# A Griffin-style hybrid layer on one core: other SBUF places for two groups of weights, a prologue that finishes token tile 0 first, and one rounding of a projection block moved

## The chip, the cores and the metric

The kernel runs on one core of one Trainium2 chip. The metric is the device time of one execution in microseconds. The core's engines are called PE (matmul; PEld is its weight load), DVE (vector), ACT (scalar), POOL (GpSimd) and SP (which here only issues DMAs). Each works through its own instructions in order, and they wait for each other through semaphores.

## What is computed

One layer on 512 tokens of width 1024, in float32. The reference, cut to what matters:

```python
h = rms_norm(x, mix_norm_pre)
xa, ga, q, k, v, f_logit, g_a, g_b = split(h @ w_in)
y_a = gelu(ga) * rg_lru(causal_dwconv(xa))            # 1280 wide
y_b = forgetting_attention(q, k, v, f_logit)          # 16 heads of 64
merged = sigmoid(g_a + b0) * (y_a @ w_proj_a) + sigmoid(g_b + b1) * (y_b @ w_proj_b)
x = x + rms_norm(merged @ w_out, mix_norm_post)
h = rms_norm(x, ffn_norm_pre)
gate, val = split(causal_dwconv(h @ w_up))            # 2 x 3072
x = x + rms_norm((gelu(gate) * val) @ w_down, ffn_norm_post)
```

## The kernel before

Every large product is made of three matmuls in the 32-bit format `float32r`. Each operand is split into a rounded high part and the rest: high times high, high times low, low times high (`mm3`, L216 to L219). A block of weights therefore arrives by DMA into a tile `raw`; ACT rounds it into `wh` (L172) and DVE, in the prologue POOL, subtracts to get `wl` (L175). `wpool` holds four of each. `fetch` works through the list `order` of weight blocks, and `unit(name, ahead)` takes a block and has the ones after it loaded and rounded. Outside of the blocks under `manual_schedule` a scheduler sets the place of each instruction on its engine; `tc.issue_after(i)` makes what is written under it stand behind `i`.

**Prologue** (L557 to L670, order by hand). The 512 tokens are four tiles of 128 (`xts`). For each tile ACT squares and sums (`sumsq`), DVE multiplies by the root and by the gains (`scaled(t, g)`, g being a half of the 1024 columns; result `xn`), PE transposes each half by four matmuls with the identity (`turn(t, g)`, L245, tile `tr_p`), ACT rounds the transposed half into `hh` (`evac_hi`, L249) and DVE puts the rest into `hl` (`evac_lo`, L253). The gains reach all 128 partitions by a matmul of a row of ones with the row `gone` (L590), in plain float32. `spin` is a matmul of the identity with itself, whose result nobody reads. The first useful product is `half(0, X)` (L229 to L232): block `xa0` with the first 256 tokens, X; Y are the last 256. It reads `hh` and `hl` of tiles 0 and 1, and the rounded `wh_xa0` and `wl_xa0`.

**Gates** (L906 to L960). The blocks `ma0` to `mb7` are made in pairs by Strassen's scheme, seven products of 12 matmuls of 256 columns each (`product`, L408 to L421). Their operands: products 1 and 2 (`p12`) take the plain weights `gmh0`/`gml0` (pool `gsplit0`) and `hh`/`hl`; product 3 takes `gmh1`/`gml1` (pool `gsplit1`) and the token sums `gsh3`; products 5, 6 and 7 take sums of weights (`gth`/`gtl`, in `wpool`) and token sums `gsh`/`gsl`; product 4 takes `gth`/`gtl` and `hh`/`hl`. In the steady order of `period` (L443) they run as 5, 6, 4 of the pair before, 3, `p12` of the next pair, 7. In PE's instructions the weights are the stationary operand and the tokens are streamed.

**Attention** (L1070 to L1109). A loop over eight pairs of heads, p = 0 to 7: scores of pair p from `q` and `k`, each split by `halves` into a high part on ACT (L970) and the rest on DVE (L971); transposes `pt` of pair p-1 with their copies by ACT (L1030) and DVE (L1031); `av` of pair p-1. In the last rounds the products of `pb`, the projection of the attention's result, fill PE. `pb_part(e, ks)` adds to block e, and at its first call takes its weights with one block ahead, so `pb_part(2, ...)` is what has `pb3` rounded.

**Up** (L1162 to L1476). The blocks `up0`, `up24`, `up1`, `up25`, `up2`, `up26` come first, each as two halves of 24 matmuls of 256 columns (X, later Y), with `h2h`/`h2l`; the weights of `up0` and `up24` have a pool of their own (`wfirst`). The other 42 blocks are 21 Strassen pairs as in the gates, there with the plain weights `mh0`, `mh1` and the sums `th`. **Down** (L1382 on) follows, with Strassen again.

The helper `offset(stack, n, side)` (L85) takes n bytes per partition at a place, so that what is put behind it moves by n. By the sizes of the pools the byte places within 512 of the operands that matter are: `hh`, `hl`, `gth`, `gtl`, `th`, `tl` at 0; `gsh`, `gsl`, `h2h`, `h2l`, `sh`, `sl` at 448; `gmh0`/`gml0` at 448; `gmh1`/`gml1`, `up0` and `up24` at 0; in the up stage `mh0` at 0 and `mh1` at 416. A block of 128 weights is 512 bytes wide and a stretch of 256 tokens 1024, so a place stays the same through a product.

Of the kernel before, what the change touches and what calls it, by code (L numbers as in the profile page):

```python
# [8 lines left out]
F32 = mybir.dt.float32  # L9
F32R = mybir.dt.float32r  # L10
BF16 = mybir.dt.bfloat16
AF = mybir.ActivationFunctionType
ALU = mybir.AluOpType
# [50 lines left out]
def kernel(  # L64
# [421 lines left out]
    with ExitStack() as rg:  # L486
        rt, ixt, tt = {}, {}, {}
        last_act = [None]
        with ExitStack() as r0:
# [68 lines left out]
            with tc.tile_pool(name="pre", bufs=2, side="right", reuse_waits="tile") as pre, ExitStack() as wp:  # L558
# [6 lines left out]
                gone = pre.tile([1, D + P], F32, name="gone", bufs=1)  # L565
                pool.memset(gone[:, D:], 1.0)
                act.dma_start(gone[:, :D], gains[0:1, :])
# [21 lines left out]
                for i in range(2):  # L589
                    pe.matmul(pgain[i], gone[:, D:], gone[:, 512 * i : 512 * i + 512], start=True, stop=True)  # L590
# [18 lines left out]
                def scaled(t, g):  # L609
                    c = HALVES[g]  # L610
                    dve.scalar_tensor_tensor(out=xns[t][:, c], in0=xts[t][:, c], scalar=rss[t], in1=pgain[g],
                                             op0=ALU.mult, op1=ALU.mult)

                def turn(t, g):
                    ptr[t, g] = turn_block(xns[t], t, g, "p")
# [11 lines left out]
                scaled(0, 0)  # L627
                sumsq(1)
                us[0].hi()
                us[0].lo(pool)  # L630
                scaled(1, 0)
                turn(0, 0)
                spin(3)
                turn(1, 0)
                scaled(0, 1)
                turn(0, 1)
                evac_hi(0, 0)
                evac_lo(0, 0)
                scaled(1, 1)
                turn(1, 1)  # L640
                evac_hi(1, 0)
                evac_lo(1, 0)
                evac_hi(0, 1)
                evac_lo(0, 1)
                evac_hi(1, 1)
                evac_lo(1, 1)
                half(0, X)
# [259 lines left out]
    with ExitStack() as g2:  # L907
# [9 lines left out]
        hfstk.close()  # L917
        st0pool = splitstk.enter_context(tc.tile_pool(name="gsplit0", bufs=2, side="right", reuse_waits="tile"))
        offset(splitstk, 448, "right")
# [43 lines left out]
    with ExitStack() as at:  # L963
# [47 lines left out]
        def pt(p, pts):  # L1011
# [10 lines left out]
            for j in range(2):  # L1022
                h = 2 * p + j
                th = apool.tile([P, PO[NT]], F32R, tag="PTh", name=f"PTh{h}")
                tl = apool.tile([P, PO[NT]], F32R, tag="PTl", name=f"PTl{h}")
                thv, tlv = (a.rearrange("p (i h c) -> p i h c", h=2, c=HD) for a in (th, tl))
                for i0, i1, src, o in ((0, 8, tbs[j], 0), (8, 10, rest, P * j)):
                    for half in range(2):
                        ps = src[half][:, o : o + (i1 - i0) * HD].rearrange("p (i c) -> p i c", c=HD)
                        act.copy(thv[:, i0:i1, half], ps)  # L1030
                        dve.tensor_tensor(out=tlv[:, i0:i1, half], in0=ps, in1=thv[:, i0:i1, half].bitcast(F32), op=ALU.subtract)  # L1031
                res.append((th, tl))
# [23 lines left out]
        def pb_part(e, ks):  # L1056
            if e not in pb:
                pb[e] = bank(f"pb{e}")
                pbw[e] = unit(f"pb{e}", 1)
            wh, wl = pbw[e]  # L1060
            for k in ks:
                mm3(pb[e], wh[:, k], wl[:, k], yb[k][:, 0], yb[k][:, 1], k == 0, k == KD - 1)

        rounded = []
# [76 lines left out]
    offset(fstk, 96)  # L1141
# [19 lines left out]
    with ExitStack() as mix:  # L1161
        wfpool = mix.enter_context(tc.tile_pool(name="wfirst", bufs=2, reuse_waits="tile"))  # L1162
        npool = mix.enter_context(tc.tile_pool(name="norm", bufs=2, reuse_waits="tile"))
        special["up0"] = special[f"up{JF}"] = wfpool
# [129 lines left out]

    ypool = fstk.enter_context(tc.tile_pool(name="ff", bufs=3, reuse_waits="tile"))
# [429 lines left out]
```

## Time and profile before

| | us |
|---|---|
| three runs | 915.5, 914.26, 915.56; median 915.5 |
| the profiled execution: its own time | 915.62 |
| its span, from the first to the last instruction | 913.8 |
| around the span | 1.8 |
| mean granted clock of PE | 0.998 |

The page's other lines stand in the prediction where they are used. Its times are microseconds from the span's start unless a column says ns. In a timeline a row gives start, duration, engine, line, operation, what it writes and reads, and in brackets how long the engine had been idle and what ended that. Matmuls are pipelined: a row's duration is longer than the distance to the next matmul's start, and it is the distances that add up to the time. L12 is line 12 of the kernel before.

### The profile page before, as it was taken

How to read it: one execution, taken by the hardware profiler on the slowest of the kernel's cores; microseconds unless marked ns; L12 is line 12 of the kernel's file. 1: busy time of each engine (PE TensorE's matmuls, PEld its weight loads, DVE VectorE, ACT ScalarE, POOL GpSimd, SP SyncE). 2: the span in 40 equal slices, each digit the busy share in tenths (PEclk: the TensorE clock that was granted, in tenths of full speed). 3: DMA queues.
4: the chain of work that ended last, by engine and by line, in shares of the span. 5: the costliest groups of instructions: out<-in, count | busy, mean ns of one | idle time of the engine just before them, and what ended most of it. 6: DMA issues, size and time to landing. Idle time of an engine off the chain costs nothing.

```text
span 913.8 us, 15945 instructions
## 1 busy us (share of the span) xinstructions
PE 904.4 (99%) x5906; PEld 805.5 (88%) x5906; DVE 726.0 (79%) x1197; ACT 601.6 (66%) x1041; POOL 218.9 (24%) x281
## 2 busy tenths in 40 slices
PE   8999999999999999999999999999999999999997
PEld 7988888887899998888888889999999999988886
DVE  4966359737777649888878588989999999889897
ACT  6565496423377757677654477878888888677664
POOL 4134444534111112212104200132323223100000
PEclk9999999999999999999999999999999999999999
DMA  7677669989968767435424654468988888699764
GB/s 261 234 214 207 191 166 274 256 229 182 212 164 198 199 222 261 180 128 174 139 93 156 208 180 160 116 174 201 231 227 209 236 210 211 205 397 328 243 200 148
DMA packets 72048, 187.86 MB, mean 206 GB/s; under 512 B 7265, under 2 KB 27793, under 8 KB 71586
## 3 DMA queue, kind: packets, MB, share of 16 engines
q1 hardware_dynamic: 47648, 127.72, 41.9%
q0 software_dynamic: 24176, 58.99, 29.8%
q8 instruction: 46, 0.75, 0.3%
q14 instruction: 32, 0.26, 0.1%
q10 hardware_dynamic: 146, 0.14, 0.0%
HBM read 150.69 MB, written 35.73 MB: 204 GB/s over the span
## 4 chain that ended last, share of the span: by engine, by line
PE 96%; DVE 1%; DMA 1%; ACT 1%; SPq 0%; issue 0%; DVEq 0%; ACTq 0%
PE up L421 7%; PE up L419 7%; PE up L418 7%; PE dn L1434 4%; PE dn L1432 4%; PE dn L1433 4%; PE pa L217 2%; PE ga L218 2%; PE ga L217 2%; PE pa L219 2%; PE pa L218 2%; PE ga L219 2%; PE k L217 2%; PE q L217 2%; PE wo L1151 2%; PE pb L217 2%
## 5 line engine op out<-in xcount | busy, mean ns | idle before, releaser
L1309 DVE SCALAR_TENSOR_TENSOR u<-up,cpt,u 128x511 f32<-128x511 f32 x96 | 71.3, 746 | 3.5 <-ACT u L1303 1.8
L362 POOL DMA_DIRECT2D ml<-raw_up x41 | 35.3, 861 | 152.6 <-ACT ml L361 89.5
L1434 PE MATMUL dn<-wh_dn,al 128*128 128x512 f32 (+1 forms) x180 | 67.7, 376 | 0.0
L1433 PE MATMUL dn<-wl_dn,ah 128*128 128x512 f32 (+1 forms) x180 | 67.5, 375 | 0.0
L1432 PE MATMUL dn<-wh_dn,ah 128*128 128x512 f32 (+1 forms) x180 | 67.5, 375 | 0.0
L419 PE MATMUL up<-sl,th 128*128 128x256 f32 x252 | 60.2, 276 | 0.0
L418 PE MATMUL up<-sh,th 128*128 128x256 f32 x252 | 60.2, 276 | 0.0
L175 DVE TENSOR_TENSOR wl_dn<-raw_dn,wh_dn 128x1024 fp32r<-128x1024 f32 x42 | 51.3, 1222 | 9.3 <-ACT wh_dn L172 9.2
L172 ACT CAST wh_dn<-raw_dn 128x1024 fp32r<-128x1024 f32 x42 | 44.1, 1050 | 21.2 <-PE dn L1434 7.3
L1303 ACT ACTIVATE u<-up,cpt 128x512 f32<-128x512 f32 x48 | 36.9, 778 | 21.6 <-PE up L421 11.6
L324 DVE TENSOR_TENSOR tl<-t,th 128x1024 fp32r<-128x1024 f32 x42 | 51.0, 1217 | 0.0
L419 PEld LDWEIGHTS up<-sl,th 128*128 128x128 f32 x252 | 47.3, 188 | 0.0
L418 PEld LDWEIGHTS up<-sh,th 128*128 128x128 f32 x252 | 47.3, 188 | 0.0
L1317 POOL TENSOR_TENSOR yf<-u,u 128x512 f32<-128x512 f32 x23 | 31.4, 1365 | 63.3 <-issue 48.8
L400 ACT CAST th<-t 128x1024 fp32r<-128x1024 f32 x42 | 43.8, 1045 | 3.3 <-DVE t L324 0.8
L418 PE MATMUL up<-h2h,mh 128*128 128x256 f32 x168 | 40.2, 276 | 0.0
L419 PE MATMUL up<-h2l,mh 128*128 128x256 f32 x168 | 40.2, 276 | 0.0
L1434 PEld LDWEIGHTS dn<-wh_dn,al 128*128 128x128 f32 x180 | 33.9, 188 | 6.8 <-DVE al L324 0.7
L1433 PEld LDWEIGHTS dn<-wl_dn,ah 128*128 128x128 f32 x180 | 33.9, 188 | 6.1
L1432 PEld LDWEIGHTS dn<-wh_dn,ah 128*128 128x128 f32 x180 | 33.9, 188 | 6.0
L421 PE MATMUL up<-sh,tl 128*128 128x256 f32 x252 | 38.8, 276 | 0.0
L998 ACT ACTIVATE P<-P,mx 128x384 f32<-128x384 f32 (+3 forms) x64 | 35.2, 553 | 4.2 <-DVE mx L993 3.3
(717 smaller groups left out, 3239.1 us busy)
## 6 DMA issues: line engine op xcount, KB each, us to landing
raw_up<-in_w_up_dram SPq DMA_DIRECT2D x48, 512.0 KB, 5.4
td<-in_w_down_dram POOLq DMA_DIRECT2D x36, 512.0 KB, 6.0
raw_dn<-td SPq DMA_DIRECT2D x24, 512.0 KB, 5.2
B<-cnd POOLq DMA_DIRECT2D x16, 640.0 KB, 5.5
ml<-raw_up POOLq DMA_DIRECT2D x20, 512.0 KB, 5.8
raw_dn<-in_w_down_dram SPq DMA_DIRECT2D x18, 512.0 KB, 4.3
raw_wo<-in_w_out_dram SPq DMA_DIRECT2D x16, 512.0 KB, 3.9
td<-td POOLq DMA_DIRECT2D x12, 512.0 KB, 10.6
```

The costliest lines, as they stand in the source:

```text
L172: act.copy(self.wh, self.raw)
L175: engine.tensor_tensor(out=self.wl, in0=self.raw, in1=self.wh.bitcast(F32), op=ALU.subtract)
L217: pe.matmul(dst, ah, bh, start=first, stop=False)
L324: dve.tensor_tensor(out=out, in0=a, in1=b, op=ALU.subtract)
L400: act.copy(self.th[i], self.t[i])
L418: pe.matmul(dst, wh[:, k], ah[:, k], start=first and k == 0, stop=False, skip_group_check=True)
L419: pe.matmul(dst, wh[:, k], al[:, k], start=False, stop=False, skip_group_check=True)
L421: pe.matmul(dst, wl[:, k], ah[:, k], start=False, stop=k == KH - 1, skip_group_check=True)
L1309: dve.scalar_tensor_tensor(out=c[:, s:], in0=ps[:, : S - s], scalar=col(C_CFW + 3 * e + j), in1=c[:, s:], op0=ALU.mult, op1=ALU.add)
L1432: pe.matmul(d[:, x], ah[:, k, tok], wh[:, k, x], start=first, stop=False, skip_group_check=True)
L1433: pe.matmul(d[:, x], ah[:, k, tok], wl[:, k, x], start=False, stop=False, skip_group_check=True)
L1434: pe.matmul(d[:, x], al[:, k, tok], wh[:, k, x], start=False, stop=last, skip_group_check=True)
```

## The change

Four places of the program differ. In the prologue, the gains go to the partitions as two `float32r` products (high part and rest, split by DVE) in place of one plain one; tile 0 is scaled, turned and rounded whole before tile 1; and the first half of `xa0` runs all its high-by-high matmuls, then high-by-low, then low-by-high. In the gates the pool `gsplit0` moves by 384 bytes and the distance between the two pools shrinks as much, so that `gmh0`/`gml0` come to place 64 within 512 and `gmh1`/`gml1` stay. For the up stage the two first blocks get a pool each with 96 bytes between them, and `x2t` moves down by 96, so that `up0` comes to place 416 and `up24` stays at 0 (it moves by 4096). In the attention the load and rounding of `pb3` are put behind the last of ACT's copies of `pt(6)`.

```diff
-                gone = pre.tile([1, D + P], F32, name="gone", bufs=1)
-                pool.memset(gone[:, D:], 1.0)
-                act.dma_start(gone[:, :D], gains[0:1, :])
+                gone = pre.tile([1, D], F32, name="gone", bufs=1)
+                act.dma_start(gone, gains[0:1, :])
...
-                for i in range(2):
-                    pe.matmul(pgain[i], gone[:, D:], gone[:, 512 * i : 512 * i + 512], start=True, stop=True)
+                one = xpool.tile([P, S], F32R, tag="xc", name="one")[0:1, :P]
+                pool.memset(one.bitcast(F32), 1.0)
+                for i, c in enumerate(HALVES):
+                    gh, gl = (xpool.tile([P, S], F32R, tag=x, name=f"gain_{x}{i}")[0:1] for x in ("xh", "xl"))
+                    dve.tensor_copy(out=gh, in_=gone[:, c])
+                    dve.tensor_tensor(out=gl, in0=gone[:, c], in1=gh.bitcast(F32), op=ALU.subtract)
+                    for j, g in enumerate((gh, gl)):
+                        pe.matmul(pgain[i], one, g, start=j == 0, stop=j == 1)
...
                 sumsq(0)
                 scaled(0, 0)
+                scaled(0, 1)
+                turn(0, 0)
+                turn(0, 1)
+                spin(3)
                 sumsq(1)
+                evac_hi(0, 0)
+                evac_hi(0, 1)
                 us[0].hi()
                 us[0].lo(pool)
-                scaled(1, 0)
-                turn(0, 0)
-                spin(3)
-                turn(1, 0)
-                scaled(0, 1)
-                turn(0, 1)
-                evac_hi(0, 0)
-                evac_lo(0, 0)
-                scaled(1, 1)
-                turn(1, 1)
-                evac_hi(1, 0)
-                evac_lo(1, 0)
-                evac_hi(0, 1)
-                evac_lo(0, 1)
-                evac_hi(1, 1)
-                evac_lo(1, 1)
-                half(0, X)
+                for g in range(2):
+                    scaled(1, g)
+                    turn(1, g)
+                for g in range(2):
+                    evac_lo(0, g)
+                for g in range(2):
+                    evac_hi(1, g)
+                    evac_lo(1, g)
+                wh, wl = us[0].parts()
+                for w, h in ((wh, hh), (wh, hl), (wl, hh)):
+                    for k in range(KD):
+                        pe.matmul(pss[0][:, X], w[:, k], h[:, k, X], start=w is wh and h is hh and k == 0, stop=w is wl and k == KD - 1)
...
         hfstk.close()
+        offset(splitstk, 384, "right")
         st0pool = splitstk.enter_context(tc.tile_pool(name="gsplit0", bufs=2, side="right", reuse_waits="tile"))
-        offset(splitstk, 448, "right")
+        offset(splitstk, 64, "right")
         st1pool = splitstk.enter_context(tc.tile_pool(name="gsplit1", bufs=2, side="right", reuse_waits="tile"))
...
-                        act.copy(thv[:, i0:i1, half], ps)
+                        copied[p] = act.copy(thv[:, i0:i1, half], ps)
...
-                pbw[e] = unit(f"pb{e}", 1)
+                with ExitStack() as held_back:
+                    if e == 2:
+                        held_back.enter_context(tc.issue_after(copied[KD - 2].ins))
+                    pbw[e] = unit(f"pb{e}", 1)
...
     fstk = ctx.enter_context(ExitStack())
-    offset(fstk, 96)
     xpool = fstk.enter_context(tc.tile_pool(name="x2", bufs=1, reuse_waits="tile"))
...
-        wfpool = mix.enter_context(tc.tile_pool(name="wfirst", bufs=2, reuse_waits="tile"))
+        wfpools = [mix.enter_context(tc.tile_pool(name="wfirst0", bufs=1, reuse_waits="tile"))]
+        offset(mix, 96)
+        wfpools.append(mix.enter_context(tc.tile_pool(name="wfirst1", bufs=1, reuse_waits="tile")))
...
-        special["up0"] = special[f"up{JF}"] = wfpool
+        special["up0"], special[f"up{JF}"] = wfpools
...
+    offset(fstk, 96)
     ypool = fstk.enter_context(tc.tile_pool(name="ff", bufs=3, reuse_waits="tile"))
```

On the engines this moves little else. In the prologue, ACT's instructions before the change (`sd_p1` is the root of tile 1, `tr_p_t_g` the transposed half g of tile t):

```order
L598 ACTIVATE xn1_195,s2_p1_196<-xt1_146 128x512 x2
L236 ACTIVATE sd_p1_201<-ss_p1_199,epst_77 128x1
L172 CAST wh_xa0_154<-raw_xa0_153 128x1024
L249 CAST hh_114<-tr_p_0_0_208 128x4x128
L249 CAST hh_114<-tr_p_1_0_216 128x4x128
L249 CAST hh_114<-tr_p_0_1_222 128x4x128
L249 CAST hh_114<-tr_p_1_1_230 128x4x128
```

and with it:

```order
L603 ACTIVATE xn1_220,s2_p1_221<-xt1_145 128x512 x2
L236 ACTIVATE sd_p1_226<-ss_p1_224,epst_77 128x1
L249 CAST hh_114<-tr_p_0_0_207 128x4x128
L249 CAST hh_114<-tr_p_0_1_212 128x4x128
L172 CAST wh_xa0_153<-raw_xa0_152 128x1024
L249 CAST hh_114<-tr_p_1_0_235 128x4x128
L249 CAST hh_114<-tr_p_1_1_241 128x4x128
```

The two casts of tile 0 now stand ahead of the rounding of `xa0`'s weights. On DVE, before:

```order
L600 TENSOR_TENSOR ss_p0_188<-s2_p0_185 128x1
L238 RECIPROCAL rs_p0_192<-sd_p0_190 128x1
L611 SCALAR_TENSOR_TENSOR xn0_184<-xt0_145,rs_p0_192,gain0_180 128x512
L600 TENSOR_TENSOR ss_p1_199<-s2_p1_196 128x1
L238 RECIPROCAL rs_p1_203<-sd_p1_201 128x1
L611 SCALAR_TENSOR_TENSOR xn1_195<-xt1_146,rs_p1_203,gain0_180 128x512
L611 SCALAR_TENSOR_TENSOR xn0_184<-xt0_145,rs_p0_192,gain1_181 128x512
L253 TENSOR_TENSOR hl_115<-tr_p_0_0_208,hh_114 128x4x128
L611 SCALAR_TENSOR_TENSOR xn1_195<-xt1_146,rs_p1_203,gain1_181 128x512
```

and with the change:

```order
L592 CAST gain_xh0_183<-gone_141 1x512
L593 TENSOR_TENSOR gain_xl0_184<-gone_141,gain_xh0_183 1x512
L592 CAST gain_xh1_189<-gone_141 1x512
L593 TENSOR_TENSOR gain_xl1_190<-gone_141,gain_xh1_189 1x512
L605 TENSOR_TENSOR ss_p0_199<-s2_p0_196 128x1
L238 RECIPROCAL rs_p0_203<-sd_p0_201 128x1
L616 SCALAR_TENSOR_TENSOR xn0_195<-xt0_144,rs_p0_203,gain0_179 128x512
L616 SCALAR_TENSOR_TENSOR xn0_195<-xt0_144,rs_p0_203,gain1_180 128x512
L605 TENSOR_TENSOR ss_p1_224<-s2_p1_221 128x1
L238 RECIPROCAL rs_p1_228<-sd_p1_226 128x1
L616 SCALAR_TENSOR_TENSOR xn1_220<-xt1_145,rs_p1_228,gain0_179 128x512
L616 SCALAR_TENSOR_TENSOR xn1_220<-xt1_145,rs_p1_228,gain1_180 128x512
```

Four instructions on the single row of gains are new at the head, and the second half of tile 1 no longer stands behind a subtraction that waits for ACT. On ACT in the attention, before, around the rounding of `pb3`:

```order
L1030 CAST PTh11_5178<-pt10_r0_5126 128x2x64
L1030 CAST PTh11_5178<-pt10_r1_5127 128x2x64
L172 CAST wh_pb3_5537<-raw_pb3_5536 128x1024
L970 CAST h_k7_5223<-k7_5188 128x512
L1048 COPY ytmp5_5228<-av10_5229 64x512
```

and with the change, 20 rows further on:

```order
L1037 CAST PTh13_5407<-pt12_r0_5355 128x2x64
L1037 CAST PTh13_5407<-pt12_r1_5356 128x2x64
L172 CAST wh_pb3_5553<-raw_pb3_5552 128x1024
L1055 COPY ytmp6_5440<-av12_5441 64x512
L1055 COPY ytmp6_5440<-av13_5452 64x512
```

The rounding of `pb3` no longer stands ahead of that of `k7`; the subtraction for `wl_pb3` on DVE moves in the same way, from ahead of `l_k7` to behind the last `PTl13`. The sequence of SP's DMAs is unchanged.

2 lines of the change are left out of this document (1 added, 1 removed).

## The prediction

> **What bounds the kernel now.** First the page's busy shares and its chain of waits, then who waited for whom.
>
> ```profile
> PE 904.4 (99%) x5906; PEld 805.5 (88%) x5906; DVE 726.0 (79%) x1197; ACT 601.6 (66%) x1041; POOL 218.9 (24%) x281
> PE 96%; DVE 1%; DMA 1%; ACT 1%; SPq 0%; issue 0%; DVEq 0%; ACTq 0%
> PE tr_p L245 <- DVE xn L611: 1.2, 1, 1.2
> ```
>
> PE is busy 99% of the span, and 96% of the chain that ended last is PE. Its only wait on another engine's data that the list of waits shows is 1.2 us in the prologue. So a gain can come from three places: useful matmuls that start earlier, matmuls that follow each other more closely, and small stalls that "busy" hides because matmuls overlap. The change touches all three. I read, in this order, the start of the chain of waits, the timeline of the first 17 us, and then the distances between equal matmuls in the gates and the up stage.
>
> **Part 1: the prologue.** The start of the chain of waits (start, duration, what):
>
> ```profile
> 2.98 6.92 DMA raw_xa<-in_w_in_dram
> 9.92 1.04 ACT wh_xa L172
> ...
> 12.88 1.11 PE tr_p L245 x4
> ```
>
> and from the timeline of the same stretch:
>
> ```profile
> 3.50 3.78 PE L590 MATMUL gain<-gone 1*128 1x512 f32 x4
> 9.49 0.29 ACT L236 ACTIVATE sd_p<-ss_p,epst 128x1 f32<-128x1 f32 x1 [0.23 <-DVE ss_p L600]
> 10.02 1.41 DVE L611 SCALAR_TENSOR_TENSOR xn<-xt,rs_p,gain 128x512 f32<-128x512 f32 x2
> 10.82 3.18 PE L245 MATMUL tr_p<-ident,xn 128*128 128x128 f32 x12 [1.22 <-DVE xn L611]
> 10.87 0.58 ACT L249 CAST hh<-tr_p 128x512 fp32r<-128x512 f32 x1
> 13.65 0.56 PE L229 MATMUL xa<-hh,wh_xa 128*128 128x256 f32 x1
> 14.01 0.41 PE L230 MATMUL xa<-hl,wh_xa 128*128 128x256 f32 x1
> 16.57 0.38 PE L230 MATMUL xa<-hl,wh_xa 128*128 128x256 f32 x1
> 16.91 0.28 PE L230 MATMUL xa<-hl,wh_xa 128*128 128x256 f32 x1
> ```
>
> Useful work begins at 13.65, when the last four transposes (from 12.88) are through. They wait for the second half of tile 1, which on DVE stands behind a subtraction that waits for ACT's cast.
>
> With the change DVE begins with four one-row instructions. Their prices come from the nearest rows, a two-input subtraction of 512 columns and a one-input operation on 16 rows:
>
> ```profile
> L507 DVE TENSOR_TENSOR xl<-xc,xh 128x512 fp32r<-128x512 f32 x10 | 6.9, 692 | 2.9 <-ACT xh L506 2.8
> L274 DVE TENSOR_SCALAR f_d<-f_y 16x512 f32<-16x512 f32 x1 | 0.4, 415 | 0.2 <-ACT f_y L272 0.2
> ```
>
> The gains have landed by 3.50, since PE reads them then. So DVE is through by 3.5 + 2 x (0.415 + 0.692) = 5.7. Then tile 0 has its sum, root and reciprocal (0.3 each at most, by the root's row), two scalings (1.41) and the last four transposes (0.21 apart): done by about 9. Nothing is paid for that, since ACT can only go on after tile 1's root, at 9.49 + 0.29 = 9.78. That root waits for tile 1's landing and does not move.
>
> From there, ACT: two casts of tile 0 (0.58 us each at most, so to 10.9), the weights' cast (1.04, to 12.0; they landed by 9.92), then tile 1's first cast. DVE: both halves of tile 1 in a row, 10.02 to 11.43. PE: four transposes from 10.82, four more right behind. Eight transposes without a gap, at 0.21 us each plus the first one's start-up, end at about 12.6. Tile 1's first cast runs at about 12.0 to 12.6. The first useful matmul then starts at about 12.6, **1.05 us earlier**. The new order of its 24 matmuls keeps the late inputs away: the first four need only the first halves, the low parts are asked for 8 matmuls later, `wl_xa0` 16 later.
>
> What 1.05 us is worth depends on PE's pace there. From 14.01 to 16.57 twelve matmuls take 2.56 us, 0.213 each; from 16.8 on they show 0.28 instead of 0.41 us and follow at about 0.12. If the switch to the quick pace keeps its place at 16.8, the 1.05 us hold 4.9 slow matmuls, each of which saves only 0.12 later: 0.58 us. If it moves with the work, it is all of 1.05. I take 1.05, because PE is now occupied without a gap from 10.82 on, where it had one just before 12.88; both ends go into the range. The Trainium skill ("TensorE: Matmul & The Clock Gate", Part 1) says that the clock is released after a busy window of about 3.4 us that runs free of the kernel. The two paces fit; whether the window's edge moves cannot be seen in one trace. By that rule a single run can get either value.
>
> **Part 2: the gates' weights.** Rows of the PE timeline in the gates, four low-by-high matmuls that close a product of 12 each; the distance from one row to the next is one product. The last row is a group of mean durations (ns):
>
> ```profile
> 273.29 0.62 PE L421 MATMUL ma<-gsh,gtl 128*128 128x256 f32 x4
> 274.65 0.62 PE L421 MATMUL ma<-gsh,gtl 128*128 128x256 f32 x4
> ...
> 282.98 0.64 PE L421 MATMUL ma<-gsh,gtl 128*128 128x256 f32 x4
> 284.40 0.63 PE L421 MATMUL ma<-gsh,gtl 128*128 128x256 f32 x4
> ...
> 288.59 0.62 PE L421 MATMUL ma<-hh,gml 128*128 128x256 f32 x4
> 289.95 0.62 PE L421 MATMUL ma<-hh,gml 128*128 128x256 f32 x4
> 291.34 0.64 PE L421 MATMUL ma<-gsh,gtl 128*128 128x256 f32 x4
> ...
> L418 PE MATMUL mb<-gsh,gth 128*128 128x256 f32 x48 | 11.8, 281 | 0.0
> ```
>
> From product 5 to product 6 it took 1.36 us in one period and 1.42 in the next, with the same shapes and the same places: 113 against 118 ns a matmul. So there are two paces, and PE keeps the one it is in. It changes at the seam from `p12` to product 7: 1.36 up to 289.95, slower from there. At that seam the streamed tokens minus the weights go from place 0-448 to 448-0 (mod 512: from 64 to 448). The up stage, where nearly all products stand at 448-0, keeps 113 throughout. With the change `p12` has 0-64, again 448, so the relation no longer turns at the seam. I expect the quick pace to last through 7, 5 and 6.
>
> In the timeline the slow 7, 5, 6 come in six of the periods (the group of `mb`'s first halves has 281 ns over 48, where a quick one has 276): 6 x 36 = 216 matmuls. In the first cycle `p12` is slow and 7, 5, 6 are quick; without the turn those 36 would stay slow. The price of a matmul is read more sharply in Part 3: 117.9 - 113.3 = 4.6 ns. Sum: (36 - 216) x 4.6 ns = **-0.82 us**. Bounds: 0 if the seam still turns the pace; -1.4 if the first cycle is quick too (216 and its 84 slow ones, 300 x 4.6).
>
> The Trainium skill speaks against this part. "TensorE: Matmul & The Clock Gate", Part 2, step 1, says that matmul and weight load have independent read ports, so that loading does not slow the running matmul. By it a place is worth nothing and Parts 2 and 3 come to zero. The rows above differ in pace with nothing but the history differing, so this trace does not bear it out; that the place decides is my inference, and the zero is kept as a rival.
>
> **Part 3: the first up blocks.** Groups of eight that close 24 matmuls, the page's group of mean durations below them:
>
> ```profile
> 557.58 1.10 PE L232 MATMUL up<-h2h,wl_up 128*128 128x256 f32 x8
> 560.41 1.10 PE L232 MATMUL up<-h2h,wl_up 128*128 128x256 f32 x8
> ...
> 587.08 1.07 PE L232 MATMUL up<-h2h,wl_up 128*128 128x256 f32 x8
> 589.80 1.07 PE L232 MATMUL up<-h2h,wl_up 128*128 128x256 f32 x8
> ...
> L421 PE MATMUL up<-sh,ml 128*128 128x256 f32 x84 | 13.1, 278 | 0.0
> L418 PE MATMUL up<-h2h,mh 128*128 128x256 f32 x168 | 40.2, 276 | 0.0
> ```
>
> 2.83 / 24 = 117.9 ns in the first halves, 2.72 / 24 = 113.3 in the second. `up0` at 416 gets the relation of `mh1` in the Strassen pairs (448-416), whose rows show 278 ns, between 276 quick and 281 slow; and what follows `mh1` there, `p12` in the last row, is quick. So `up24` and `up1`, 48 matmuls, should turn quick: -0.22 us; `up0`'s second half pays 24 x 3 ns = 0.07. Together **-0.15 us**, between 0 and -0.25.
>
> **Part 4: `pb3`.** ACT, DVE, SP and PE around it; the last four rows are two rounds' scores:
>
> ```profile
> 453.51 1.05 ACT L172 CAST wh_pb<-raw_pb 128x1024 fp32r<-128x1024 f32 x1 [2.47 <-PE k L218]
> 455.74 0.68 DVE L971 TENSOR_TENSOR l_k<-k,h_k 128x512 fp32r<-128x512 f32 x1
> 455.85 0.34 SPq L166 DMA_DIRECT2D raw_pb<-in_w_proj_b_dram  x1
> 488.00 0.33 SPq L166 DMA_DIRECT2D raw_wo<-in_w_out_dram  x1
> 469.25 0.58 ACT L1048 COPY ytmp<-av 64x512 f32<-64x512 f32 x1 [1.70 <-PE av L1045]
> 438.86 0.49 PE L984 MATMUL s12c<-h_k,h_q 64*128 64x512 f32 x1
> 439.43 0.39 PE L984 MATMUL s12c<-h_k,l_q 64*128 64x512 f32 x1
> 456.11 0.50 PE L984 MATMUL s14c<-h_k,h_q 64*128 64x512 f32 x1
> 456.81 0.39 PE L984 MATMUL s14c<-h_k,l_q 64*128 64x512 f32 x1
> ```
>
> `l_k7` ends at 456.42, after the scores of round 7 began, and these take 0.70 us to the third product where round 6 took 0.57. Without `pb3` ahead of it `l_k7` is ready over a microsecond earlier: **-0.13 us**. The moved cast fits ACT's idle 1.70 us ahead of 469.25, where it needs 1.05; if it did not, `av`'s copy would be late by the overhang, 0.1 at most. DVE's 1.2 us subtraction may push `y` by as much; PE has the transposes of the next round in between. The load of the last `pb` block, which takes over `pb3`'s raw buffer, moves from 455.85 to about 470; behind it on SP nothing is issued until 488.00, so it lands long before its use.
>
> **Sum.** -1.05 - 0.82 - 0.15 - 0.13 = -2.15. The profiled execution took 915.62 (span 913.8 and 1.8 around it), so 913.5; the runs' median is 915.5, 0.1 below it: **913.4 us**. As PE is bound to the end, each term reaches it.
>
> **The rivals.**
> - *The places give nothing.* The seam turns the pace whatever the relation, because at the seam itself weights at 0 are loaded while tokens at 0 are streamed, before and after. For it: that address stays. Against it: product 4 streams 0 on 0 all along and product 3 after it is quick. Left are Parts 1 and 4: 915.5 - 1.18 = 914.3.
> - *More than forecast.* The first cycle of the gates is quick too (-0.55), and the quick clock comes a stretch earlier, since PE is dense from 10.82: of the 3.15 us from 13.65 to 16.8 nearly half is saved, -1.0. 911.9. Against it: it needs both.
> - *Slower: the up stage falls into the 118 ns pace.* `up0`, now in another relation, runs directly ahead of `up24` and the 21 pairs. If `up24` comes out slow and the pace sticks, a pair's 72 matmuls outside of product 3 cost 0.33 us; beyond 6 pairs the gain is gone, over all 21 it is +7.0: 920.4. Against it: after every product 3, which has the same relation, `p12` was quick (276 ns over 168).
>
> **How the numbers follow.** The forecast gets 0.58 (its own range 912.6 to 914.2, from the halves of Parts 1 and 2), the places that give nothing 0.22, more 0.12, the slow up stage 0.08. About 0.2%, 1.8 us, is what a measurement of this kernel can tell from no change; the line lies at 913.7, close to the forecast. So faster: four fifths of 0.58, all of 0.12, a tenth of 0.22: 0.60. Same: the rest of these, 0.32. Slower: 0.08. The range reaches from the case of more to the places that give nothing with a Part 1 at its lower bound: 911.8 to 914.9.
>
> **What would show it.** The first `L653` or `L229` useful matmul at about 12.6 instead of 13.65, and where its pace turns to 0.12. In the gates, distances of 1.36 between the rows of products 7, 5 and 6 from the second cycle on; 1.42 there refutes Part 2. In the up stage 2.72 from `up24` to `up1`, and 113 ns kept to the end. In round 7 the third score product 0.57 after the first. I am wrong on the whole if the start stays at 13.65, or if the products of the up stage take 1.42.

## The result and the profile after

The changed kernel takes **912.8 us** (median of 19 runs) against 914.4 for the kernel before (19 runs beside it): a ratio of **0.9978, 95% interval 0.9972 to 0.9985**, so 2.0 us gained, 1.4 to 2.6 (the medians differ by 1.6). Run again beside the experiments it gave 912.4 against 914.3, ratio 0.9984 (0.9976 to 0.9992). The forecast was 913.4.

The two profiled executions differ by more, 915.62 and 912.11. To see where, I subtract the start of each PE instruction in one trace from the start of the same instruction in the other and note where the difference changes. The ledger of after minus before: -2.45 to the first useful matmul, -1.17 inside `xa0`, +0.32 in the second halves of `xa0` to `xa2`, -0.09 in the gates, -0.10 in the scores of round 7 and +0.10 in those of round 1, +0.2 in the up stage, and -0.36 in one block of the down stage.

Below, the page of the changed kernel and its list of PE's waits. PE is as full as before. The prologue's wait has kept its length, but 0.9 us of it now lies ahead of tile 0's transposes and 0.2 ahead of tile 1's (the brackets of the PE rows further down), and there is a wait in the up stage that the list of the kernel before did not have.

```profile
PE 900.5 (99%) x5906; PEld 803.4 (88%) x5906; DVE 728.1 (80%) x1201; ACT 601.6 (66%) x1041; POOL 219.5 (24%) x281
...
PE 97%; ACT 1%; DVE 1%; DMA 1%; issue 0%; SPq 0%; DVEq 0%; ACTq 0%
...
PE tr_p L245 <- DVE xn L616: 1.1, 2, 0.9
PE tr_f L260 <- DVE xn L1206: 0.5, 1, 0.5
```

**Prologue.** First the landing of tile 1 as ACT sees it (the square that ends its wait), before and after:

```profile
8.54 0.63 ACT L598 ACTIVATE xn<-xt 128x512 f32<-128x512 f32 x1 [2.21 <-DMA xt<-in_x_dram]
```

```profile
7.51 0.63 ACT L603 ACTIVATE xn<-xt 128x512 f32<-128x512 f32 x1 [1.53 <-DMA xt<-in_x_dram]
...
8.46 0.29 ACT L236 ACTIVATE sd_p<-ss_p,epst 128x1 f32<-128x1 f32 x1 [0.23 <-DVE ss_p L605]
```

and the PE timeline of the changed kernel:

```profile
6.48 1.97 PE L245 MATMUL tr_p<-ident,xn 128*128 128x128 f32 x8 [0.91 <-DVE xn L616]
8.24 1.34 PE L584 MATMUL xa<-ident 128*128 128x128 f32 x6
9.79 1.31 PE L245 MATMUL tr_p<-ident,xn 128*128 128x128 f32 x8 [0.21 <-DVE xn L616]
11.20 1.31 PE L653 MATMUL xa<-hh,wh_xa 128*128 128x256 f32 x8
12.36 1.23 PE L653 MATMUL xa<-hl,wh_xa 128*128 128x256 f32 x8
13.42 1.10 PE L653 MATMUL xa<-hh,wl_xa 128*128 128x256 f32 x8
```

In this execution tile 1's rows landed 1.03 us earlier than in the profile before. Nothing shows that this is the change: in fourteen profiles of kernels with the same loads they were there anywhere from 6.3 to 8.5 us (7.5 to 8.5 in the three with the old prologue, 6.3 to 8.2 in the others, 7.5 and 6.9 for the changed kernel itself). So the start has to be counted from the end of tile 1's root: 13.65 - 9.78 = 3.87 us before, 11.20 - 8.75 = 2.45 after. The second thing is the pace. The eight transposes from 6.48 take 1.97 us, the eight from 9.79 take 1.31: PE has turned quick before the first useful matmul, seven microseconds earlier than before (16.8).

**Gates.** The low-by-high rows again, in the order `p12` (two), 7, 5, 6, 4, 3, `p12`:

```profile
276.81 0.63 PE L421 MATMUL ma<-hh,gml 128*128 128x256 f32 x4
...
278.21 0.62 PE L421 MATMUL ma<-gsh,gtl 128*128 128x256 f32 x4
...
279.57 0.62 PE L421 MATMUL ma<-gsh,gtl 128*128 128x256 f32 x4
...
280.93 0.62 PE L421 MATMUL ma<-gsh,gtl 128*128 128x256 f32 x4
...
285.13 0.63 PE L421 MATMUL ma<-hh,gml 128*128 128x256 f32 x4
...
286.54 0.64 PE L421 MATMUL ma<-hh,gml 128*128 128x256 f32 x4
```

Products 7, 5 and 6 are now 1.36 us apart, as forecast; but the two halves of `p12` are 1.41 apart where they were 1.36.

**First up blocks**, the last eight matmuls of `up0`, `up24`, `up1`, and then the transposes of tile 2:

```profile
554.24 1.10 PE L232 MATMUL up<-h2h,wl_up 128*128 128x256 f32 x8
...
556.99 1.07 PE L232 MATMUL up<-h2h,wl_up 128*128 128x256 f32 x8
...
559.71 1.07 PE L232 MATMUL up<-h2h,wl_up 128*128 128x256 f32 x8
561.23 1.03 PE L260 MATMUL tr_f<-ident,xn 64*128 64x64 f32 x16 [0.45 <-DVE xn L1206]
```

`up24` and `up1` are quick (2.72 from row to row). But from 559.71 to the first transpose 1.52 us pass, where eight matmuls need 0.9: DVE's `xn` of tile 2 is late.

**`pb3`.** Scores of round 7, the first and the third product; on ACT the moved cast and the next copy of `av`:

```profile
452.86 0.49 PE L991 MATMUL s14c<-h_k,h_q 64*128 64x512 f32 x1
...
453.43 0.39 PE L991 MATMUL s14c<-h_k,l_q 64*128 64x512 f32 x1
...
463.99 1.05 ACT L172 CAST wh_pb<-raw_pb 128x1024 fp32r<-128x1024 f32 x1
...
465.61 0.59 ACT L1055 COPY ytmp<-av 64x512 f32<-64x512 f32 x1 [0.57 <-PE av L1052]
```

0.57 us as in round 6, where it was 0.70; and behind the cast ACT still waits for `av`.

### The profile page after: what moved, and what is told of

The parts are those of the page before. It is cut to its first block, busy times and chain, and to the rows that moved or that the text cites. A ratio compares the mean times of both kernels' runs of the same rounds, so it can differ in the third digit from the quotient of the medians.

```text
span 910.3 us, 15947 instructions
## 1 busy us (share of the span) xinstructions
PE 900.5 (99%) x5906; PEld 803.4 (88%) x5906; DVE 728.1 (80%) x1201; ACT 601.6 (66%) x1041; POOL 219.5 (24%) x281
## 4 chain that ended last, share of the span: by engine, by line
PE 97%; ACT 1%; DVE 1%; DMA 1%; issue 0%; SPq 0%; DVEq 0%; ACTq 0%
PE up L418 7%; PE up L419 7%; PE up L421 7%; PE dn L1446 4%; PE dn L1445 4%; PE dn L1444 4%; PE ga L219 2%; PE ga L217 2%; PE pa L219 2%; PE pa L218 2%; PE pa L217 2%; PE ga L218 2%; PE k L217 2%; PE q L217 2%; PE pb L217 2%; PE k L219 2%
## 5 line engine op out<-in xcount | busy, mean ns | idle before, releaser
L421 PE MATMUL up<-sh,tl 128*128 128x256 f32 x252 | 38.8, 276 | 0.0
```

Source lines behind the costliest of these rows:

```text
L421: pe.matmul(dst, wl[:, k], ah[:, k], start=False, stop=k == KH - 1, skip_group_check=True)
```

## The experiments

Two questions: which part of the change brings the gain, and whether the quick pace comes early through the change or by luck. Many of these kernels share what stands behind the prologue, so each trace also tells something of the rest.

**Each half alone.** `e1_prologue` is the kernel before with the change's first part only (its diff hunks from `gone` to `half(0, X)`), `e2_rest` the kernel before with the other three.

> The kernel before with Part 1 alone (prologue). Theory D (density): the reorder lets the first useful matmul start about 1.4 us sooner after tile 1's root than before (3.87 us after the root's end in the trace before, 2.45 in the trace after), and PE, dense from the first transpose on, gets the quick pace before 11.2 us instead of at 16.8, worth up to 1.2 more: -1.2 to -2.6 us against before, nearly all of the whole change's -1.6. Rival P (as predicted): start -1.05 and the switch of the pace moves with the work, -1.05. Rival L (luck): the earlier start in the trace after was only an early landing of tile 1; from root to first useful matmul it takes 3.4 us or more, and the time falls by less than 0.5.

> The kernel before with Parts 2, 3 and 4 and the old prologue. Theory D: gates: p12 at 118 ns and products 7, 5, 6 at 113, net -0.05 us a period, -0.2 to -0.4 in all; the first up blocks gain 0.35 us from 118 to 113 ns and give 0.5 back as a wait of the transposes for xn; pb3 -0.1. Together -0.6 to 0. Rival P (as predicted): -0.82 - 0.15 - 0.13 = -1.10, with p12 quick. In the trace: p12's distance between its two halves 1.42 us by D, 1.36 by P.

`e1_prologue`: 912.9 against 914.8 us, ratio 0.9983 (0.9974 to 0.9992): 1.6 us gained, 0.7 to 2.4. Its profile, the root of tile 1 and then PE:

```profile
9.06 0.29 ACT L236 ACTIVATE sd_p<-ss_p,epst 128x1 f32<-128x1 f32 x1 [0.23 <-DVE ss_p L605]
...
10.39 1.69 PE L245 MATMUL tr_p<-ident,xn 128*128 128x128 f32 x8 [0.43 <-DVE xn L616]
12.18 1.32 PE L653 MATMUL xa<-hh,wh_xa 128*128 128x256 f32 x8
```

The first useful matmul is 12.18 - 9.35 = 2.83 us behind the root, **1.04 less** than before. The pace turned at 11.6, within the transposes, so all 24 matmuls of `xa0` are quick: -1.28 in the ledger. Of that 0.32 is given back, since the second halves of `xa0` to `xa2` come out at 118 ns a matmul instead of 113. Together -2.0 in the prologue of this trace, in reach of the measured -1.6. Later stretches of the same execution lose again (0.8 in the up stage and 0.4 in the down stage above all), so that its span of 913.3 is only 0.5 below the 913.8 of the profile before: the times, not this one span, carry the result.

`e2_rest`: 914.7, ratio 0.9995 (0.9984 to 1.0005), so no gain that the times show. Its trace has the gates at -0.41 (-0.27 in `ma`, -0.14 in `mb`), `pb3` at -0.10, and between `up0` and `up25` nothing. The -0.4 of the gates in rows of L421, as above:

```profile
278.50 0.63 PE L421 MATMUL ma<-hh,gml 128*128 128x256 f32 x4
...
279.92 0.63 PE L421 MATMUL ma<-hh,gml 128*128 128x256 f32 x4
...
281.31 0.62 PE L421 MATMUL ma<-gsh,gtl 128*128 128x256 f32 x4
...
282.67 0.62 PE L421 MATMUL ma<-gsh,gtl 128*128 128x256 f32 x4
```

1.42 within `p12`, 1.36 from 7 to 5: the same exchange as in the changed kernel.

**Is it density that turns the pace?** Two kernels in which only idle products differ, the spins whose result nobody reads:

```diff
                 turn(0, 0)
-                spin(3)
+                spin(5)
```

is `e3_spin5`, made from the kernel before, and

```diff
                 turn(0, 1)
-                spin(3)
                 sumsq(1)
```

is `e4_no_spin`, made from the changed kernel.

> The kernel before with one number changed: 5 idle products instead of 3 behind tile 0's first transposes, so that PE is busy from 8.1 to about 10.5 where it stood idle from 9.6 to 10.82. Theory D: the pace of PE turns quick after a stretch in which PE is nearly always busy; so it turns at about 13 us instead of 16.8, some 12 to 15 matmuls fall from 0.213 to 0.118 us, -0.6 to -1.5 us with the start unchanged at 13.65. Rival F: the switch comes at a time that the kernel does not set; median time unchanged within 0.4, and the switch near 16.8 or anywhere.

> The changed kernel without the 3 idle products between tile 0's and tile 1's transposes, so PE stands idle from about 8.2 to 9.8 us. Theory D: the quick pace comes only after the useful work has begun (13 to 17 us instead of before 11.2): the first useful matmul at the same distance from tile 1's root, about 0.5 us more for slow transposes, then 10 to 24 matmuls at 0.213 instead of 0.118: 0.8 to 2.3 us slower than the changed kernel. Rival F: the idle products do not matter, the same time within 0.4 us.

`e4_no_spin` gave 914.6 us, ratio to the kernel before 1.0002 (0.9991 to 1.0012): without six idle matmuls the whole gain of the change is gone. Its PE rows:

```profile
6.43 1.97 PE L245 MATMUL tr_p<-ident,xn 128*128 128x128 f32 x8 [0.87 <-DVE xn L616]
10.17 1.97 PE L245 MATMUL tr_p<-ident,xn 128*128 128x128 f32 x8 [1.77 <-DVE xn L616]
11.95 2.08 PE L652 MATMUL xa<-hh,wh_xa 128*128 128x256 f32 x8
13.84 1.91 PE L652 MATMUL xa<-hl,wh_xa 128*128 128x256 f32 x8
15.54 1.42 PE L652 MATMUL xa<-hh,wl_xa 128*128 128x256 f32 x8
```

The start is still early (11.95, 2.82 us behind the root), but eight matmuls take 1.9 us and PE turns quick only at 16.2. So the earlier start alone is worth little: what starts earlier in the slow pace runs at half speed. From the root to the end of these 24 matmuls it is 7.67 us against 8.19 before, 0.5 less, which the times do not show.

`e3_spin5` gave 914.5, ratio 0.9997 (0.9988 to 1.0006): -0.6 or more was expected, and -1.1 to +0.5 is what the interval allows. In its trace the mechanism is there, PE turning at 12.4 and no useful matmul slow; but the old order then met DVE, and the second halves of the `xa` blocks gave 0.32 back here too. So the times show no gain for the early turn alone either (their interval leaves room for one of up to 1.1 us); only both together, in `e1_prologue`, show one:

```profile
10.24 2.55 PE L245 MATMUL tr_p<-ident,xn 128*128 128x128 f32 x12
12.54 0.36 PE L229 MATMUL xa<-hh,wh_xa 128*128 128x256 f32 x1
...
14.19 0.39 PE L230 MATMUL xa<-hl,wh_xa 128*128 128x256 f32 x1 [0.27 <-DVE hl L253]
```

All fourteen profiles together (times from the span's start; "landed" is ACT's start on tile 1's second half; slow are useful matmuls started before PE turned):

| kernel | landed | root's end | first useful | behind root | PE turned | slow |
|---|---|---|---|---|---|---|
| before | 8.5 | 9.78 | 13.65 | 3.87 | 16.8 | 14 |
| `e2_rest` | 8.0 | 9.23 | 13.30 | 4.07 | 16.6 | 15 |
| `e3_spin5` | 7.5 | 8.70 | 12.54 | 3.84 | 12.4 | 0 |
| `e4_no_spin` | 7.9 | 9.13 | 11.95 | 2.82 | 16.2 | 19 |
| after | 7.5 | 8.75 | 11.20 | 2.45 | 9.3-9.8 | 0 |
| `e1_prologue` | 8.1 | 9.35 | 12.18 | 2.83 | 11.6 | 0 |
| `e5_norm` | 8.2 | 9.41 | 11.86 | 2.45 | 9.8-10.4 | 0 |
| `e6_gate32` | 7.8 | 9.06 | 11.89 | 2.83 | 11.0 | 0 |
| `e7_gate416` | 7.3 | 8.54 | 11.37 | 2.83 | 12.2 | 3 |
| `e8_old_order` | 7.6 | 8.83 | 11.66 | 2.83 | 11.0 | 0 |
| `e9_again` | 6.9 | 8.17 | 11.52 | 3.35 | 11.9 | 1 |
| `e10_norm` | 8.2 | 9.45 | 12.08 | 2.63 | 11.0 | 0 |
| `e11_norm_spin` | 6.9 | 8.09 | 11.30 | 3.21 | 10.0 | 0 |
| `e12_old_gains` | 6.3 | 8.45 | 11.75 | 3.30 | 10.5 | 0 |

With the new prologue, eight transposes and at least six idle matmuls follow each other from 6.4 to 7.2 us on, 3.1 us without a gap, and PE turns between 9.3 and 12.2 whatever it waits after that (0 to 0.5 us). Where the first stretch is shorter and the gap behind it longer (`e4_no_spin` 1.8 us of transposes, then 1.8 idle; before 2.2, then 1.2; `e2_rest` 2.2, then 0.7 and another 0.3) it turns at 16 to 17. The ten profiles on the one side and the three on the other do not overlap, which leaves little room for luck. With ten idle matmuls behind four transposes and no gap at all (`e3_spin5`) it is 12.4.

A busy PE by itself is not what counts. The rows of the windows from 6.00 to 9.50, before and then after (length, PE's busy time, that of the other engines, PEclk, DMA):

```profile
6.00:9.50 3.50, 3.50 (x12) 2.10 (x10) 0.91 (x2) 1.06 (x5) 0.00 (x0) 1.00 1.00 379
...
6.00:9.50 3.50, 3.02 (x14) 2.91 (x14) 1.92 (x5) 1.76 (x5) 0.00 (x0) 1.00 1.02 402
```

Before, PE is busy without a gap from 1.49 to 9.60 and still turns only at 16.8; after, it stands idle for 0.91 us ahead of 6.48 and turns at 9.3 to 9.8. From 3.50 to 7.28 PE was busy with the gains' products before, which have one row of 128 (`1*128` in their row). In these traces they did not bring the turn, and the dense 128-row matmuls did; why is not shown.

**Places, order, a new wait.** Four kernels with one execution each, all made from the changed kernel:

`e5_norm` keeps what `rstd_of` issues on ACT in `roots`, issues tile 2's second norm ahead of tile 3's, and holds tile 3's squares behind tile 2's root (the last of the three is shown, the others are left out):

```diff
-                act.activation(out=xn[:, c], in_=x2t[:, t, c], func=AF.Square, accum_out=s3[:, i : i + 1])
+                with ExitStack() as behind_root:
+                    if t == 3:
+                        behind_root.enter_context(tc.issue_after(roots["f2"].ins))
+                    act.activation(out=xn[:, c], in_=x2t[:, t, c], func=AF.Square, accum_out=s3[:, i : i + 1])
```

`e6_gate32` moves one place; `e7_gate416` has 32 and 416 in the two lines:

```diff
-        offset(splitstk, 384, "right")
+        offset(splitstk, 416, "right")
...
-        offset(splitstk, 64, "right")
+        offset(splitstk, 32, "right")
```

and `e8_old_order` gives the first half of `xa0` its old order:

```diff
-                wh, wl = us[0].parts()
-                for w, h in ((wh, hh), (wh, hl), (wl, hh)):
-                    for k in range(KD):
-                        pe.matmul(pss[0][:, X], w[:, k], h[:, k, X], start=w is wh and h is hh and k == 0, stop=w is wl and k == KD - 1)
+                half(0, X)
```

> The changed kernel with one thing more: ACT takes the root of tile 2's second norm ahead of tile 3's squares, so that DVE's xn of tile 2 starts about 1 us sooner. In the trace after, the transposes of tile 2 waited 0.5 us for that xn behind up1, which had turned quick. Theory W (new wait): the distance from the last matmul of up1 to the first transpose falls from 0.73 to 0.21 us and no tr_f wait is left in the list of waits; up24 and up1 stay at 113 ns. Theory S (the stall set the pace): without it up25 to the second half of up24 come out at 118 ns, 9 blocks of 24 matmuls, +1.0 us that eats the 0.5. Rival: the pace behind the transposes is not set by the wait; 113 or 118 whatever the wait is.

> The changed kernel with gmh0 and gml0 at place 32 (mod 512) instead of 64; tokens of p12 stay at 0, so tokens minus weights is 480 instead of 448. Theory R (a distance of 32 alternates and leaves the next product quick, as product 3 of the up pairs does with 448-416): p12 about 116.6 ns a matmul with unequal neighbours, products 7, 5 and 6 at 113 in every period; ma and mb together 0.1 to 0.2 us shorter than in the trace after. Rival F (the seam from p12 to 7 flips whatever pace p12 had): where p12 is quick 7, 5, 6 are slow and the other way round, at every place.

> The changed kernel with gmh0 and gml0 at place 416, tokens minus weights 96. Theory R: only the distance modulo 64 matters; 96 is 32 off as 480 is, so p12 at about 116.6 ns and 7, 5, 6 at 113. Rival Q (the distance itself counts): p12 at 113 or 118 throughout as at 64 and 448, and 7, 5, 6 in the other pace.

> The changed kernel with xa0's first half in the old order (high and low products of one k in turn) instead of all wh x hh first. As predicted: the first useful matmul keeps its distance of about 2.5 us to tile 1's root, but the second waits for DVE's hl of tile 1 (the four subtractions ended at about 11.5 to 12.8 in the trace after, 2.1 us and more behind the first xn), so xa0's 24 matmuls take about 0.5 to 0.7 us longer than the 3.16 us in the trace after. Rival: DVE is through in time, the same 3.2 us, and the order is worth nothing.

The one execution of each took 911.6, 912.9, 913.4 and 913.6 us in this order, beside 916.8 for one of the kernel before. Nineteen executions of the kernel before spread over 3.4 us, so these times separate nothing, and what follows is read from the traces.

The gates first. From the starts of the records, the mean distance of one matmul to the next (ns), in the steady periods:

| place of `gmh0` | `p12` | 7 | 5 | 6 | 4 | 3 |
|---|---|---|---|---|---|---|
| 448 (before) | 113.4 | 117.9 | 117.8 | 117.8 | 119.2 | 114.9 |
| 64 (after, `e2_rest`) | 117.6 | 114.9 | 113.3 | 113.3 | 118.4 | 115.3 |
| 32 (`e6_gate32`) | 118.2 | 114.3 | 113.3 | 113.3 | 118.4 | 115.3 |
| 416 (`e7_gate416`) | 119.8 | 115.1 | 113.3 | 113.3 | 118.3 | 115.3 |

Theory R fell: a distance of 32 does not alternate here, and `p12` is slow at all three new places, each at its own pace (so rival Q of `e7_gate416`, 113 or 118, fell as well). What is common to the steady periods is that 7, 5 and 6 come out in the other pace than `p12`, as rival F had it. In the first cycle that rule has exceptions: 5 and 6 follow a `p12` of 117.7 there and stay at 117.6 and 117.8 in the kernel before (117.9 and 117.8 behind a `p12` of 119 to 120 in `e7_gate416`), while behind a slow `p12` they are quick in the trace after. One piece of the trace after follows the rule as well: two matmuls of `mb0` took 0.23 us each for no reason that shows, `p12` went on at 113, and 7, 5 and 6 of that period came out at 118. Why the seam turns the pace stays open.

`e8_old_order`: the first useful matmul is 2.83 us behind the root, as in `e1_prologue`, but the second comes 0.72 us after it, waiting for `hl`, and `xa0` takes 3.54 us (11.66 to 15.20) against 3.04 in `e1_prologue` and 3.16 after. In the profiles with the new order and no slow useful matmul the block took 2.95 to 3.17, so the order is worth 0.4 to 0.6.

```profile
11.66 0.39 PE L229 MATMUL xa<-hh,wh_xa 128*128 128x256 f32 x1 [0.15 <-ACT hh L249]
12.38 0.39 PE L230 MATMUL xa<-hl,wh_xa 128*128 128x256 f32 x1 [0.34 <-DVE hl L253]
```

`e5_norm`: no `tr_f` wait is left in the list, the ledger against the trace after has -0.52 at the end of `up1` and -0.32 in the transposes, and the blocks behind stay at 113. So theory S fell in this execution, and in `e10_norm` and `e11_norm_spin` too. The end of `up1` and the transposes of tile 2:

```profile
560.01 1.07 PE L232 MATMUL up<-h2h,wl_up 128*128 128x256 f32 x8
561.01 0.71 PE L262 MATMUL tr_f<-ident,xn 64*128 64x64 f32 x16
```

1.00 us from row to row instead of 1.52. Counted from `up0`, `up25` starts at 8.98 us in the three profiles with this fix, at 9.83 and 9.68 in the two of the changed kernel, and at 9.46 before. Whether `up25` to the second half of `up24` (216 matmuls, 1.0 us between the two paces) run at 113 or 118 differs from execution to execution: quick from `up2` on in the trace before but slow in `e1_prologue` and `e3_spin5`, whose up stage is the same; with `up0` at 416 quick in seven and slow in four (`e2_rest`, `e4_no_spin`, `e7_gate416`, `e8_old_order`). What decides it is open; the wait does not, since at the same 0.3 us it is quick in `e9_again` and slow in `e4_no_spin`.

**Timed side by side.** The changed kernel again (`e9_again`), the fix of the wait (`e10_norm`), the fix with more spins (`e11_norm_spin`):

```diff
                         pe.matmul(pgain[i], one, g, start=j == 0, stop=j == 1)
+                spin(2)
...
-                spin(3)
+                spin(4)
```

and the changed kernel with the gains as before (`e12_old_gains`):

```diff
...
-                for i, c in enumerate(HALVES):
...
-                    for j, g in enumerate((gh, gl)):
-                        pe.matmul(pgain[i], one, g, start=j == 0, stop=j == 1)
+                for i in range(2):
+                    pe.matmul(pgain[i], gone[:, D:], gone[:, 512 * i : 512 * i + 512], start=True, stop=True)
```

> The changed kernel itself once more, beside the next three. 0.9978 of before, 912.8 us, again. Theory D (a dense PE brings the quick pace early): first useful matmul 2.45 to 2.83 us behind tile 1's root, and at most 4 of the useful matmuls at 0.213 us. Rival L (luck): 10 or more of them slow in this execution.

> The changed kernel with the root of tile 2's second norm ahead of tile 3's squares (the kernel of the one look before). Theory W: the wait of 0.3 to 0.9 us ahead of tile 2's transposes is gone in the trace, and 0.3 to 0.8 us of the time with it, 912.0 to 912.5. Rival: the wait only moves to tile 3's transposes or to the products behind them; the same time as the changed kernel.

> The kernel before it with 2 idle products behind the gains' and 4 instead of 3 between tile 0's and tile 1's transposes, so that PE is busy from 5.4 us on with gaps of 0.5 us at most. Theory D: the quick pace comes before 12 us in every execution, no useful matmul is slow, spread of the runs smaller, 0 to 0.4 us faster than the kernel before it. Rival: the idle products stand in the way of tile 1's transposes where its rows land early; 0.1 to 0.4 us slower.

> The changed kernel with the gains' products as before (two float32 products with 1 row, which ended at 7.2 us, instead of four float32r ones, which ended at 5.4). As predicted in Part 1: tile 0 is not what the start waits for; its transposes begin at 7.2 instead of 6.4 to 6.7, the first useful matmul stays 2.45 to 2.83 us behind tile 1's root, and the time is the changed kernel's within 0.4. Theory D adds: dense for 0.7 us less, so perhaps a few slow useful matmuls more, up to +0.4. Rival: late tile 0 holds back ACT's casts and the start by up to 0.7.

| | median us | ratio to before | 95% interval |
|---|---|---|---|
| `e9_again` | 912.4 | 0.9984 | 0.9976 to 0.9992 |
| `e10_norm` | 911.2 | 0.9972 | 0.9962 to 0.9983 |
| `e11_norm_spin` | 912.2 | 0.9978 | 0.9969 to 0.9987 |
| `e12_old_gains` | 913.2 | 0.9995 | 0.9985 to 1.0005 |

`e10_norm` has the lowest median of all kernels here; between it and the changed kernel the intervals overlap, so the 1.1 us of the medians is not proved, and the 0.7 to 0.85 us that `up25` starts sooner in the traces is the better figure. It came out below the 912.0 to 912.5 that were expected. More spins gained nothing further (0.95 us above `e10_norm` by the medians, the intervals overlap), though PE turned at 10.0 and the runs spread less (911.2 to 912.7 against 911.8 to 915.0): tile 1 had landed early, and its transposes waited behind the idle products, 3.21 us from root to first useful matmul.

`e12_old_gains` went against what was expected of the time: 0.85 us above the changed kernel by the medians (the intervals overlap). Its trace shows a way in which tile 0 can hold the start after all:

```profile
7.31 0.75 DVE L611 SCALAR_TENSOR_TENSOR xn<-xt,rs_p,gain 128x512 f32<-128x512 f32 x1 [0.86 <-PE gain L590]
7.97 0.15 DVE L600 TENSOR_TENSOR ss_p<-s_p 128x1 f32<-128x1 f32 x1
8.16 0.29 ACT L236 ACTIVATE sd_p<-ss_p,epst 128x1 f32<-128x1 f32 x1 [1.14 <-DVE ss_p L600]
```

DVE waited 0.86 us for the second gain, and tile 1's sum stood behind it on DVE; ACT waited 1.14 us to take its root. Tile 1 had landed at 6.3 and gained nothing by it.

## Why the prediction was right, and where its steps were not

The time of 912.8 lies within the range and within the forecast's own; the gain, 2.0 us and the second time 1.5, stands against 2.1 forecast. That the sum agrees is in part luck, because the errors of its terms cancel: Part 1 was worth more than its 1.05, Part 2 half of its 0.82, and Part 3 cost time in most executions. The list of waits had one line more than the prediction said, 1.5 us in which the first idle products waited for POOL's `ident`; none of the terms rests on it.

**Part 1, the start: right.** 1.05 us earlier was predicted; behind the same root it is 1.04 (`e1_prologue`, and four more profiles at 2.82 or 2.83), 1.42 where the transposes already run quick.

**Part 1, its worth: too small.** The step "if the switch to the quick pace keeps its place ..., 0.58; if it moves with the work, ... 1.05" took the end of the slow pace as something that stands still or shifts by as much as the work. It went from 16.8 to 9.3 - 12.2, since finishing tile 0 first puts eight transposes and the spins next to each other. Measured 1.6 (0.7 to 2.4) by time, 2.0 in the trace. The rival "more", given 0.12, had density as its reason, but counted it from 10.82 on, and expected 1.0 more from it. `e4_no_spin` speaks against that version: dense from 10.17 on, PE still turned only at 16.2, with the turn 7.1 us behind the root as before (7.0), and the trace gained 0.5 as in the prediction's other case (0.58). It is the stretch from 6.4 to 7.2 on that brings the early turn, and without that turn the times show nothing gained. The Trainium skill ("TensorE: Matmul & The Clock Gate", Part 1) has the clock released after a busy window of about 3.4 us that runs free of the kernel. The table agrees that the kernel does not set the moment alone: the turn comes 2.8 to 6.3 us after the start of the stretch that brings it, and in two executions of the changed kernel itself after 2.8 and 5.2. It does not agree that 3.4 us of a busy PE are enough, as the 8.1 us before 9.60 in the kernel before show. How full a window must be, and of what, is not in the table.

**Part 1, "nothing is paid" for tile 0:** right where tile 1 lands late. Where it lands at 7 us or earlier, tile 0 is in the way: its spins on PE in `e9_again` and `e11_norm_spin` (3.2 to 3.35 us from root to start), and with the old gains its scaling on DVE too. The four gain products, costed at nothing, bring tile 0 forward by 0.5 to 0.8 us and so are worth something in such executions.

**Part 2: half.** -0.82 predicted, -0.41 measured in `e2_rest`. The failed step is "with the change `p12` has 0-64, again 448, so the relation no longer turns at the seam". The seam turns it still in the steady periods; what changed is that `p12` enters it slow. The 216 matmuls of 7, 5 and 6 did turn quick (-0.86 with product 7 at 114.9), product 4 and the first cycle brought another 0.2, and the 144 matmuls of `p12` that became slow, 4.2 ns each, took 0.6 back. The rule of the Trainium skill that speaks against this part (same page, Part 2, step 1: independent read ports) would make a place worth nothing, and that does not hold in these traces: the same matmul takes 113.4, 117.6, 118.2 or 119.8 ns as the weights stand at 448, 64, 32 or 416. Whether the ports are the reason is not shown.

**Part 3: the matmuls right, the sum wrong.** `up24` and `up1` turned quick, -0.21. But DVE's `xn` of tile 2 had been just in time for PE in the slow pace, and the wait for it took 0.1 to 0.9 us in the profiles with the new place and without the fix. From `up0` to `up25` that is between 0 (`e2_rest`) and 0.8 us (`e6_gate32`) lost where -0.15 was forecast. The old place is not free of it either: `e3_spin5`, whose up stage is that of the kernel before, lost 0.3 there. The failed step is that the prediction named no work that this stretch waits for next; `e5_norm` takes the wait away, and `up25` then starts 0.5 us sooner than before.

**Part 4: right.** -0.10 against -0.13, and the moved cast disturbed nothing.

Of the rivals, the slow up stage did not occur in any profile with the new place: from the first Strassen pair on, the median distance of the matmuls is 113 ns in every profile, whatever the blocks before them did. The milder form of it, 216 matmuls at 118 ns ahead of the pairs, came in four of those eleven profiles, but also in two of the three with the old place.

## What to carry to other kernels

Count a prologue from its data's landing and look for the moment at which PE turns quick: an earlier start in the slow pace was worth little here (0.5 us in the trace of `e4_no_spin`, nothing that its times show), and with a stretch of full-height matmuls without gaps, filled with idle products, ahead of it 1.6 us. But each idle product also stands in the queue ahead of the data that lands early. A pace that hangs on places and on history cannot be moved at one product without reading what its neighbours then do. And when a stretch of PE is made quicker, look which engine was just in time for it.

## What the runs showed that was not expected

- The granted clock of the profile does not show the slow pace of the start. In the table of windows of the kernel before, PEclk (the third number from the end) is 1.00 in the very window in which the first useful matmuls follow each other every 0.213 us instead of 0.118:

```profile
13.00:16.50 3.50, 3.50 (x17) 3.50 (x18) 1.81 (x3) 2.88 (x5) 1.30 (x2) 1.00 1.04 383
```

- Two traces of the same instructions differ by up to 1 us in the up stage alone, since 216 matmuls keep either 113 or 118 ns, and by single stalls and waits of 0.2 to 0.9 us at other places in each execution (0.8 for one wait in the gates of `e10_norm`, 0.7 between the down stages of `e1_prologue` and of the changed kernel). One pair of profiles could not have shown a 2 us change; here it showed 3.5.
